# Row-free SSM quantities ahead of the first product, the norm's factors by a product with ones, and a plain second feed-forward product

## The chip, the cores and the metric

One core of one Trainium2 chip runs the whole kernel. The metric is the device time of one launch in microseconds (us); a figure given for a kernel is the median of its runs.

## What is computed

One layer of a hybrid encoder, on 512 rows of width 1024 in fp32: three residual sub-layers. Cut to what matters here:

```python
h = rms_norm(x, norm_mix_g)                    # 512 x 1024
p = h @ w_in                                   # q | k | v | conv input (512) | u (256)
o_sb   = stick_breaking_attention(q, k, v)     # 8 heads of 64
o_conv = conformer_conv(p[..., s3:s4], ...)
o_ssm  = s5_ssm(p[..., s4:], lam_re, lam_im, log_dt, b, c, d, glu_w)
x = x + mixed @ w_out
x = x + memory_cross_attention(rms_norm(x), rms_norm(mem), ...)
hf = rms_norm(x, norm_ffn_g)
gate, up = split(hf @ ffn_w_in)                # hidden width 2816
x = x + (silu(gate) * up) @ ffn_w_out          # 2816 -> 1024
```

In `s5_ssm` many quantities do not depend on the rows: the step `dt`, the decay `exp(lam dt)` with its powers, sines and cosines, and the discretised input matrix `bb` made of `fr`, `fi` and b. They depend on the parameters alone. The state scan and the outputs then use them with u.

## The kernel before

**Products.** Every large product is made in three TensorE instructions (`mm3`, L104 to L108): each operand is split into a high part, cast by ScalarE (ACT, L112), and a low part, subtracted by VectorE (DVE, L113), and high x high, high x low and low x high are summed in a PSUM bank. `load_w` (L87 to L95) fetches weights into one of three `wst` buffers and splits them in the same way (cast L93, subtraction L94).

**Order.** The order on each engine comes from a scheduler that follows the order of the program and the priorities given (`tc.high_priority`), and from pools: a tile with a tag waits until the buffers of that tag are free. PSUM has eight banks in three tags, `acc` (4), `z` (2) and `tp` (2). The pool of split operands has four buffers of each half (`whi`, `wlo`); the split weight tiles of the feed-forward stage (`wbh`, `wbl`) have two.

**Head.** The four row tiles of x are fetched, normalised by `norm_rows` (L151 to L156: a sum of squares on ACT, a reciprocal root, and at L156 one DVE instruction that multiplies a half row by the root and by `gb`), transposed on TensorE (L165, tiles `nxp`) and split into `xnh` and `xnl`. `gb`, the norm's factors on all 128 partitions, comes by two broadcasting transfers of 256 KB each, issued between those of x (L857 to L861). Then `ssm()` (from L276) is woven by `weave` (L175) with a side chain: the convolution's input product (tiles `cv`, weights `wc0` to `wc3`), the projections for stick-breaking (`qkv`, weights `ws00` and on), and the convolution's taps. The generator `ssm` yields how much side work may go in at each point (`SSM_FILL`). Its own order before: the product for u (weights `wu0`, `wu1`), the transposes `uk` and `UT`, the row-free quantities, then `wr`, `wi`, `Qr`, `Qi` (powers times `bb` and c, L432 and L435), their transposes `wTr`, `wTi` (L446), the small products `kp` (L460) and their copies `Kf` (L464, L467), the products S (L479) and the scan.

**Middle.** Stick-breaking attention, the output projection, cross-attention and the first feed-forward product follow. The last works in 22 units with PSUM sums f...acc, f...tp and f...z on an order written out by hand (L1238). It leaves `aF[p]`, for each of 11 pairs p two hidden tiles of 128 x 512 (hidden x rows).

**Second feed-forward product** (L1250 to L1357). It takes the hidden tiles by pairs p and p + 11, cuts rows and columns into halves, and computes each 2 x 2 block product with seven products in place of eight. `shared(p)` makes four of them for all pairs, `others(p)` the other three in a second pass over the pairs. The combinations of the weights (tiles `foa`, `fob`, `foc`, `keep`) are made on GpSimd (POOL; L1276 to L1278, L1296), those of the hidden values on DVE (L1283 to L1285) and POOL (L1289). The results are added up into `xr` (L1325) by DVE and, for a part, by POOL, and stored.

Of the kernel before, what the change touches and what calls it, by code (L numbers as in the profile page):

```python
# [70 lines left out]
def layer(ctx: ExitStack, tc: tile.TileContext, A: dict, out: bass.AP, dbg=None):  # L71
# [79 lines left out]
    def norm_rows(t, xt, gb, h, hiT, loT, pool, tag, bank="tp"):  # L151

        ss = pool.tile([P, 1], F32, tag="nss", bufs=2, name=f"{tag}ss{t}")
        s.activation(h, xt, AF.Square, accum_out=ss)
        r = rstd(ss, D, pool, 1, "rn")
        rows_turn(t, h, hiT, loT, tag, bank, lambda c: v.scalar_tensor_tensor(h[:, c], xt[:, c], r, gb[:, c], op0=ALU.mult, op1=ALU.mult))  # L156
# [119 lines left out]
    def ssm(sp, sk, wu):  # L276
        def sc(name):
            o, n = SK[name]
            return sk[:, o:o + n]
# [6 lines left out]


        uT = sp.tile([P, 2, LC, NCH], F32, tag="uT", name="uT")
        pu = [ps("acc", f"u{ct}") for ct in range(2)]
        for h in range(2):  # L290
            c = slice(h * 256, h * 256 + 256)
            for ct in range(2):
                for k in range(KD):
                    o = (k % 4) * 256 + ct * P
                    mm3(pu[ct][:, c], cols(wu[k // 4], slice(o, o + P)), [x[:, k, c] for x in xn], k == 0, k == KD - 1)
        for ct in range(2):
            s.copy(uT[:, ct].rearrange("p j c -> p c j"), pu[ct].rearrange("p (c j) -> p c j", j=LC))

        uk = sp.tile([P, NST, LC, 32], F32, tag="wTr", name="uk")
        UT = sp.tile([P, NST, NCH], F32, tag="UT", name="UT")  # L300
        for ct in range(2):
            pt = ps("tp", f"uk{ct}")
            for j in range(LC):
                te.transpose(pt[:, j * P:(j + 1) * P], uT[:, ct, j, :], ident)
            v.tensor_copy(uk[:, ct * 4:ct * 4 + 4], pt.rearrange("p (j t h) -> p t j h", j=LC, h=32))
        for hf in range(2):
            pt = ps("tp", f"UT{hf}")
            for k in range(4):
                T = hf * 4 + k
                te.transpose(pt[:, k * P:(k + 1) * P], uk[:, T].rearrange("p j h -> p (j h)"), ident)  # L310
            s.copy(UT[:, hf * 4:hf * 4 + 4, :].rearrange("p t c -> p (t c)"), pt)

# [81 lines left out]
        yield SSM_FILL[0]  # L394
# [25 lines left out]
        v.tensor_tensor(bb[:, 1], b1, b2, op=ALU.add)  # L420
        halves = [(slice(i * 64, i * 64 + 64), slice(i * 16, i * 16 + 16)) for i in range(2)]
# [426 lines left out]
    with tc.tile_pool(name="ssmp", bufs=1, side="right") as sp:  # L848
        sk = sp.tile([P, NSK], F32, name="sk")
        xb = [slotB("xb" + i, F32, i, 1).rearrange("p (a b) t -> p a (b t)", a=2) for i in "hl"]  # L850
        gb = sp.tile([P, D], F32, tag="wTi", name="gb")
# [5 lines left out]
        for i in range(2):  # L857
            c = slice(i * 512, i * 512 + 512)
            nc.sync.dma_start(gb[:, c], A["norm_mix_g"][c].partition_broadcast(P))
            if i == 0:  # L860
                x_rows(1)  # L861
        nc.sync.dma_start(sk, A["sk"])
        wu = [load_w(A["w_u"][:, 4 * i:4 * i + 4, :].rearrange("p k n -> p (k n)"), 1024, f"wu{i}") for i in range(2)]
# [23 lines left out]
        weave(ssm(sp, sk, wu), side)  # L887
# [152 lines left out]
    with tc.tile_pool(name="ff", bufs=1, side="right") as ff:  # L1040
# [207 lines left out]


        HF = NF // 2  # L1250
        kp = [slotA("kpa", F32, "h"), slotB("kpb", F32, "h", 0)]
        keep = [kp[p // 8][:, p % 8, :] for p in range(HF)]
        uw = slotB("uw", F32, "l", 0)

        def raw_w(p, nm):
            if p // 2 % 2 == 0:
                return ff.tile([P, 3, 512], F32, tag="wsb", bufs=2, name=nm)
            return slotB(nm, F32, "hl"[p % 2], 1)

        def w_tiles(nm):  # L1260
            return [ff.tile([P, 3, 512], F32R, tag="wb" + i, bufs=2, name=f"{nm}{i}") for i in "hl"]

        def thin(nm, w, src):

            n = src.shape[-1]
            parts = [wp.tile([P, 1024], F32R, tag="w" + i, bufs=WB, name=nm + i)[:, :w * n].rearrange("p (w n) -> p w n", n=n) for i in ("hi", "lo")]
            split(*parts, src)
            return parts

        def shared(p):  # L1270
            r = raw_w(p, f"foa{p}")
            bx = wp.tile([P, 1024], F32, tag="wst", bufs=3, name=f"fob{p}")
            b, x = bx[:, :512], bx[:, 512:].rearrange("p (w n) -> p w n", n=256)
            nc.sync.dma_start(r[:, :3:2, :], A["w_fo"][p].rearrange("p (j n) -> p j n", j=2))
            nc.sync.dma_start(b, A["w_fo"][p + HF][:, 512:])
            g.tensor_tensor(r[:, 1], r[:, 2], r[:, 0], op=ALU.subtract)  # L1276
            g.tensor_tensor(r[:, 2], b, r[:, 2], op=ALU.subtract)  # L1277
            g.tensor_tensor(keep[p], b, r[:, 1], op=ALU.subtract)  # L1278
            W = w_tiles(f"fow{p}")
            split(*W, r[:, :3])  # L1280
            T2 = thin(f"fot{p}", 1, keep[p].unsqueeze(1))
            a = aF[p]
            v.tensor_tensor(x[:, 0], a[:, 1], a[:, 3], op=ALU.add)  # L1283
            v.tensor_tensor(x[:, 1], a[:, 0], a[:, 1], op=ALU.subtract)
            v.tensor_tensor(a[:, 1], x[:, 0], a[:, 0], op=ALU.subtract)  # L1285
            X = [wp.tile([P, 4, 256], F32R, tag="w" + i, bufs=WB, name=f"foy{p}{i}") for i in ("hi", "lo")]
            split(*[y[:, :2] for y in X], a[:, :2])
            split(*[y[:, 2:] for y in X], x)
            g.tensor_tensor(a[:, 0], a[:, 2], a[:, 1], op=ALU.subtract)  # L1289
            at = lambda i: [y[:, i] for y in X]  # L1290
            return [(at(0), [y[:, 0] for y in W]), (at(1), [y[:, 0] for y in T2]), (at(2), [y[:, 1] for y in W]), (at(3), [y[:, 2] for y in W])]

        def others(p):
            r = raw_w(p + 1, f"foc{p}")
            nc.sync.dma_start(r[:, :2, :], A["w_fo"][p + HF].rearrange("p (j n) -> p j n", j=2))
            g.tensor_tensor(r[:, 2], r[:, 0], keep[p], op=ALU.subtract)  # L1296
            W = w_tiles(f"foz{p}")
            split(*W, r[:, :3])
            a = aF[p]
            X = [wp.tile([P, 1024], F32R, tag="w" + i, bufs=WB, name=f"fov{p}{i}") for i in ("hi", "lo")]  # L1300
            X0 = [y[:, :256] for y in X]
            X1 = [y[:, 256:768].rearrange("p (w n) -> p w n", n=256) for y in X]
            split(*X0, a[:, 0])
            split(*X1, a[:, 2:])
# [110 lines left out]
```

## Time and profile before

| | |
|---|---|
| median of 3 runs | 868.52 us (866.0 to 869.06) |
| the profiled execution | 867.2 us |
| its span, first to last instruction | 865.1 us |
| mean granted TensorE clock | 0.960 |
| bytes moved by DMA | 79.49 MB |

One execution was profiled. PE is TensorE's matrix work, PEld its weight loads, which overlap it; DVE, ACT and POOL are VectorE, ScalarE and GpSimd; SP issues the transfers. A window's row gives busy times in a stretch of the span; a row of waits gives the engine and line that waited and what ended the wait; a row of the timeline gives start, duration, engine, line, output and inputs, and in brackets the idle time before it and what ended that.

The stages lie in the span about so: head and SSM to about 130 us, stick-breaking attention to 260 us, then output projection, cross-attention and the first feed-forward product, and the second feed-forward product from 718.5 us to the end.

### The profile page before, as it was taken

The page shows a single profiled execution, that of the slowest core. Times are in us where ns is not written, and L with a number is a line of the kernel's source. Part 1 is how long each engine was busy: PE and PEld are TensorE (multiplying, and loading weights), DVE is VectorE, ACT ScalarE, POOL GpSimd, SP SyncE. Part 2 cuts the span into 40 slices and gives each one's busy share as a digit, 9 for nine tenths or more (in the row PEclk, how much of TensorE's full clock was granted, in tenths as well). Part 3 has the DMA queues.
Part 4 walks back from the last instruction along what each step waited for, and adds up shares of the span by engine and source line. Part 5 has one row for each costly group of instructions (what it writes and reads, how often), then busy time and mean ns, then how long its engine had stood idle before and what let it go on. Part 6 is the DMA issues. An engine that isn't in the chain of part 4 may idle for free.

```text
span 865.1 us, 12277 instructions
## 1 busy us (share of the span) xinstructions
PE 782.9 (90%) x4570; PEld 679.5 (79%) x4570; DVE 747.0 (86%) x1173; ACT 421.5 (49%) x764; POOL 295.4 (34%) x211
## 2 busy tenths in 40 slices
PE   5969999798789999999999689999999997787888
PEld 4758897685567778888888589999999995565676
DVE  6989999999697958575847997999999899999995
ACT  6423546476676746345634553434343333434542
POOL 3550000000000000000000636677777656788850
PEclk9989999898798999999999989999999999899999
DMA  7300221132420432420341122333332223232141
GB/s 258 96 27 1 73 73 56 43 122 89 136 68 25 124 120 88 133 73 25 123 146 49 46 76 99 102 118 99 122 123 98 86 74 122 73 110 82 65 158 74
DMA packets 25659, 79.49 MB, mean 92 GB/s; under 512 B 2816, under 2 KB 3072, under 8 KB 25600
## 3 DMA queue, kind: packets, MB, share of 16 engines
q1 hardware_dynamic: 25600, 78.71, 27.8%
q8 instruction: 36, 0.59, 0.3%
q14 instruction: 23, 0.19, 0.1%
HBM read 76.60 MB, written 2.10 MB: 91 GB/s over the span
## 4 chain that ended last, share of the span: by engine, by line
PE 59%; DVE 24%; POOL 5%; ACT 5%; issue 3%; DMA 3%; SPq 0%; DVEq 0%; POOLq 0%; ACTq 0%
PE xo L106 2%; PE xo L108 2%; PE xo L107 2%; PE f L107 2%; PE f L106 2%; PE f L108 2%; PE xq L106 2%; PE xq L108 2%; PE xq L107 2%; PE qkv L107 2%; POOL foa L1277 2%; PE qkv L108 2%; PE qkv L106 1%; POOL foa L1276 1%; DVE ss L694 1%
## 5 line engine op out<-in xcount | busy, mean ns | idle before, releaser
L732 POOL TENSOR_TENSOR sqa<-sqa,sq 128x512 f32<-128x512 f32 x3 | 3.9, 1286 | 255.2 <-ACT sq L731 221.6
L1124 POOL TENSOR_TENSOR wgb<-wga,wgb 128x512 f32<-128x512 f32 x22 | 42.0, 1909 | 141.5 <-DMA wga<-in_w_gu_dram 136.6
L1123 POOL TENSOR_TENSOR wgb<-wgb 128x512 f32<-128x512 f32 x20 | 35.2, 1762 | 40.8 <-DMA wgb<-in_w_gu_dram 32.0
L583 DVE SCALAR_TENSOR_TENSOR cac<-hp,pk,cac 128x512 f32<-128x512 f32 x60 | 44.4, 748 | 0.0
L1188 POOL TENSOR_TENSOR aF<-aF,fup 128x1024 f32<-128x1024 f32 x10 | 34.8, 3478 | 4.2 <-DVE fup L1184 4.2
L1140 POOL TENSOR_TENSOR wga<-wga 128x512 f32<-128x512 f32 x20 | 27.5, 1376 | 20.4 <-DVE wga L1139 20.4
L1289 POOL TENSOR_TENSOR aF<-aF 128x256 f32<-128x256 f32 x11 | 20.4, 1854 | 15.8 <-DVE foy0lo L113 4.4
L1139 DVE TENSOR_TENSOR wga<-wgb,wga 128x512 f32<-128x512 f32 x22 | 22.3, 1015 | 0.1
L1276 POOL TENSOR_TENSOR foa<-foa 128x512 f32<-128x512 f32 x11 | 17.6, 1601 | 11.2 <-DMA foa<-in_w_fo_dram 11.2
L681 PE MATMUL z<-kh,qh 64*128 64x512 f32 (+3 forms) x32 | 14.6, 456 | 7.1 <-DVE ss L695 7.1
L1277 POOL TENSOR_TENSOR foa<-fob,foa 128x512 f32<-128x512 f32 x11 | 19.7, 1794 | 0.2
L696 ACT ACTIVATE ss<-ss 128x384 f32<-128x384 f32 (+1 forms) x24 | 13.5, 562 | 12.8 <-DVE ss L695 11.9
L689 ACT ACTIVATE sa<-z 128x384 f32<-128x384 f32 (+1 forms) x24 | 12.7, 530 | 13.3 <-PE z L684 13.2
L681 PEld LDWEIGHTS z<-kh,qh 64*128 64x128 f32 x32 | 6.6, 205 | 15.4 <-DVE ss L695 6.5
L113 DVE TENSOR_TENSOR wTl<-wT,wTh 128x384 fp32r<-128x384 f32 (+2 forms) x40 | 16.4, 416 | 2.1 <-ACT wTh L112 2.0
L1186 ACT ACTIVATE aF<-aF 128x1024 f32<-128x1024 f32 x11 | 11.6, 1056 | 13.2 <-DVE aF L1182 11.0
L1296 POOL TENSOR_TENSOR foc<-foc,kpa 128x512 f32<-128x512 f32 x8 | 15.7, 1975 | 5.8 <-DMA foc<-in_w_fo_dram 4.6
L112 ACT CAST wTh<-wT 128x384 fp32r<-128x384 f32 (+2 forms) x40 | 14.7, 371 | 5.7 <-PE wT L708 3.5
L692 DVE SCALAR_TENSOR_TENSOR sa<-z,sa 128x384 f32<-128x384 f32 (+1 forms) x24 | 14.3, 597 | 3.5 <-ACT sa L691 3.3
L694 DVE TENSOR_TENSOR_SCAN ss<-ones,sa 128x512 f32<-128x512 f32 (+1 forms) x16 | 17.3, 1083 | 0.0
L708 PE MATMUL wT<-ident,ss 128*128 128x128 f32 x80 | 13.6, 291 | 1.6 <-DVE ql L116 1.4
L1283 DVE TENSOR_TENSOR fob<-aF 128x256 f32<-128x256 f32 x11 | 14.4, 1308 | 0.1
(2309 smaller groups left out, 3452.5 us busy)
## 6 DMA issues: line engine op xcount, KB each, us to landing
wgb<-in_w_gu_dram SPq DMA_DIRECT2D x22, 512.0 KB, 3.3
wga<-in_w_gu_dram SPq DMA_DIRECT2D x22, 512.0 KB, 3.4
foa<-in_w_fo_dram SPq DMA_DIRECT2D x11, 512.0 KB, 3.7
foc<-in_w_fo_dram SPq DMA_DIRECT2D x11, 512.0 KB, 3.3
fob<-in_w_fo_dram SPq DMA_DIRECT2D x11, 256.0 KB, 3.3
xr<-in_x_dram SPq DMA_DIRECT2D x4, 512.0 KB, 7.4
out_dram<-xr SPq DMA_DIRECT2D x8, 256.0 KB, 2.1
xbh<-in_x_dram SPq DMA_DIRECT2D x2, 512.0 KB, 5.0
```

Of the source, the lines that this page charges most:

```text
L106: te.matmul(o, a[0], b[0], start=start, stop=False)
L107: te.matmul(o, a[0], b[1], start=False, stop=False)
L108: te.matmul(o, a[1], b[0], start=False, stop=stop)
L583: v.scalar_tensor_tensor(a, x, w, a, op0=ALU.mult, op1=ALU.add)
L694: v.tensor_tensor_scan(ts[:, ::-1], d0, ta[:, ::-1], 0.0, op0=ALU.mult, op1=ALU.add)
L1123: eng.tensor_tensor(b[:, 0], b[:, 1], b[:, 2], op=ALU.add)
L1124: g.tensor_tensor(b[:, 1], a[:, 0], b[:, 1], op=ALU.subtract)
L1139: v.tensor_tensor(a[:, 0], b[:, 0], a[:, 0], op=ALU.subtract)
L1140: eng.tensor_tensor(a[:, 1], a[:, 1], a[:, 0], op=ALU.subtract)
L1188: (g if i + 1 < len(units) else v).tensor_tensor(aF[p], aF[p], dst, op=ALU.mult)
L1276: g.tensor_tensor(r[:, 1], r[:, 2], r[:, 0], op=ALU.subtract)
L1277: g.tensor_tensor(r[:, 2], b, r[:, 2], op=ALU.subtract)
```

## The change

Three parts.

1. **The factors.** `gb` is no longer broadcast by transfers. The 1024 factors come in one row (`grow`, 4 KB), and two matmuls of a column of ones with that row (`onesr`) spread it over 128 partitions into two PSUM banks of tag `acc`. L156 reads its factor from there. The transfers are issued in the order grow, first row tile, sk (the SSM's parameters), second row tile, wu0, wu1, third and fourth row tile; before it was first row tile, gb, second row tile, gb, sk, wu0, wu1, and the rest.
2. **The row-free quantities.** In `ssm` they stand ahead of u's product, and the generator is run to that point (`next(S5)`) right after the calls of `norm_rows`. Two tiles change their tags with it (`tmpm`, `onesr`).
3. **The second feed-forward product** becomes plain: 22 hidden tiles, eight sums of 128 rows x 512 columns in all eight PSUM banks, each hidden tile used in all of them in turn; for the last two hidden tiles sum by sum, with its addition into `xr` and its store right behind. The pairs, combinations and the second pass are gone.

```diff
-        rows_turn(t, h, hiT, loT, tag, bank, lambda c: v.scalar_tensor_tensor(h[:, c], xt[:, c], r, gb[:, c], op0=ALU.mult, op1=ALU.mult))
+        rows_turn(t, h, hiT, loT, tag, bank, lambda c: v.scalar_tensor_tensor(
+            h[:, c], xt[:, c], r, gb[c.start // 512] if isinstance(gb, list) else gb[:, c], op0=ALU.mult, op1=ALU.mult))
...
     def ssm(sp, sk, wu):
-        uT = sp.tile([P, 2, LC, NCH], F32, tag="uT", name="uT")
...
-        yield SSM_FILL[0]
...
         v.tensor_tensor(bb[:, 1], b1, b2, op=ALU.add)
+        yield 0
+
+        uT = sp.tile([P, 2, LC, NCH], F32, tag="uT", name="uT")
...
+        yield SSM_FILL[0]
...
-        gb = sp.tile([P, D], F32, tag="wTi", name="gb")
+        grow = sp.tile([1, D], F32, tag="wTi", name="grow")
+        onesr = sp.tile([1, P], F32, tag="t3", name="onesr")
+        v.memset(onesr, 1.0)
+        nc.sync.dma_start(grow, A["norm_mix_g"].unsqueeze(0))
+        gps = [ps("acc", f"gb{i}") for i in range(2)]
+        for i in range(2):
+            te.matmul(gps[i], onesr, grow[:, i * 512:i * 512 + 512], start=True, stop=True)
...
-                norm_rows(t, xb[t // 2][:, t % 2, :], gb, hn[t], xn[0], xn[1], sp, "nx", ("tp", "z")[t % 2])
+                norm_rows(t, xb[t // 2][:, t % 2, :], gps, hn[t], xn[0], xn[1], sp, "nx", ("tp", "z")[t % 2])
         dbg("xn", xn)
+        S5 = ssm(sp, sk, wu)
+        next(S5)
...
+        slots = [("acc", t, 0) for t in range(4)] + [("z", 0, 1), ("z", 1, 1), ("tp", 2, 1), ("tp", 3, 1)]
+        acc = {(t, hf): ps(tag, f"fo{t}{hf}") for tag, t, hf in slots}
+        TAIL = 2
+
+        def hidden(k):
+            p, j = k // 2, k % 2
+            X = [wp.tile([P, 1024], F32R, tag="w" + i, bufs=WB, name=f"fox{k}{i}")[:, :512] for i in ("hi", "lo")]
+            split(*X, aF[p][:, 2 * j:2 * j + 2].rearrange("p a t -> p (a t)"))
+            r = wp.tile([P, 1024], F32, tag="wst", bufs=3, name=f"for{k}")
+            nc.sync.dma_start(r, A["w_fo"][p + j * (NF // 2)])
+            W = [ff.tile([P, 3, 512], F32R, tag="wb" + i, bufs=2, name=f"fow{k}{i}").rearrange("p a n -> p (a n)")[:, :1024] for i in "hl"]
+            split(*W, r)
+            return X, W
+
+        def step(k, X, W, t, hf):
+            mm3(acc[t, hf], cols(X, slice(t * P, (t + 1) * P)), cols(W, slice(hf * 512, hf * 512 + 512)), k == 0, k == NF - 1)
+
+        for k in range(NF - TAIL):
+            ops = hidden(k)
+            for _, t, hf in slots:
+                step(k, *ops, t, hf)
+        ops = [hidden(k) for k in range(NF - TAIL, NF)]
+        for _, t, hf in slots:
+            for k in range(TAIL):
+                step(NF - TAIL + k, *ops[k], t, hf)
+            c = slice(hf * 512, hf * 512 + 512)
+            v.tensor_tensor(xr[:, t, c], acc[t, hf], xr[:, t, c], op=ALU.add)
             nc.sync.dma_start(out[t * P:(t + 1) * P, c], xr[:, t, c])
```

The first place is the start of the program on PE. The names `hnVr`, `hnVi`, `hnKf` and `hnUT` are the four normalised row tiles, `nxp` their transposes, u the SSM's input product. Before, the last two rows of the transposes of the first two row tiles and the start of u:

```order
L165 MATMUL nxp_150<-ident,hnVr 128x128
L165 MATMUL nxp_178<-ident,hnVi 128x128
L106 MATMUL u_260<-xnh,wu0h 128x256
L106 MATMUL u_261<-xnh,wu0h 128x256
L107 MATMUL u_260<-xnl,wu0h 128x256
L108 MATMUL u_260<-xnh,wu0l 128x256
```

And with the change:

```order
L862 MATMUL gb_109<-grow,onesr 128x512
L862 MATMUL gb_110<-grow,onesr 128x512
L166 MATMUL nxp_147<-ident,hnVr 128x128 x4
L166 MATMUL nxp_155<-ident,hnVr 128x128 x4
L166 MATMUL nxp_175<-ident,hnVi 128x128 x4
L166 MATMUL nxp_183<-ident,hnVi 128x128 x4
L166 MATMUL nxp_203<-ident,hnKf 128x128 x4
L106 MATMUL u_421<-xnh,wu0h 128x256
L106 MATMUL u_422<-xnh,wu0h 128x256
L166 MATMUL nxp_231<-ident,hnUT 128x128 x4
L107 MATMUL u_421<-xnl,wu0h 128x256
```

The two products that spread the factors (`gb`) stand first, the transposes of the first half of the third row tile now stand ahead of u's first matmul, and those of the fourth lie between u's matmuls.

The second place is DVE in the SSM, from the building of `Qr` to the scan; `ws02l` is the low half of a weight tile for the projections, `csg` a step of the convolution's gate, t are scratch tiles. Before:

```order
L94 TENSOR_TENSOR ws02l<-ws02s,ws02h 128x768
L435 TENSOR_TENSOR Qr<-t_521,t_522 64x8x4x16 x2
L432 TENSOR_TENSOR t_521<-ncr,api 128x512
L432 TENSOR_TENSOR t_522<-sk,apr 128x512
L435 TENSOR_TENSOR Qi<-t_521,t_522 64x8x4x16 x2
L483 TENSOR_TENSOR t_522<-S_697,E 128x512
L484 TENSOR_TENSOR t_523<-S_697,E 128x512
L144 SCALAR_TENSOR_TENSOR csg_800<-cv_592,csg_800 128x512
L467 SCALAR_TENSOR_TENSOR Kf<-ident,sk,Kf 128x128 x4
```

And with the change, from the split of `ws02` on, which now has `Qr` and `Qi` ahead of it (the lines are 5 further down):

```order
L94 TENSOR_TENSOR ws02l<-ws02s,ws02h 128x768
L472 SCALAR_TENSOR_TENSOR Kf<-ident,sk,Kf 128x128 x4
L487 TENSOR_TENSOR t_382<-S_697,E 128x512
L472 SCALAR_TENSOR_TENSOR Kf<-ident,sk,Kf 128x128 x4
L488 TENSOR_TENSOR t_383<-S_702,E 128x512
L489 TENSOR_TENSOR t_384<-S_702,E 128x512
L490 TENSOR_TENSOR t_385<-S_697,E 128x512
L491 TENSOR_TENSOR Vr<-t_382,t_383 128x512
L492 TENSOR_TENSOR Vi<-t_384,t_385 128x512
L495 SCALAR_TENSOR_TENSOR Vr<-r_266,Vr 128x128
L495 SCALAR_TENSOR_TENSOR Vi<-r_266,Vi 128x128
L144 SCALAR_TENSOR_TENSOR csg_805<-cv_597,csg_805 128x512
```

The split of `ws02` went from ahead of `Qr` to behind `Qi`, and `Kf` ahead of the first product with S; the step of `csg` comes further down, behind the scan's first rows.

The third place is DVE in the second feed-forward product; `fow` are the split weights, `fot`, `foy` and `fox` split operands, `fob` and `aF` hidden values. Before, for one pair in the first pass:

```order
L113 TENSOR_TENSOR fot4lo<-kpa,fot4hi 128x512
L1283 TENSOR_TENSOR fob_7554<-aF_6078 128x256
L1284 TENSOR_TENSOR fob_7554<-aF_6078 128x256
L1285 TENSOR_TENSOR aF_6078<-fob_7554,aF_6078 128x256
L113 TENSOR_TENSOR foy4lo<-aF_5602,foy4hi 128x512
L113 TENSOR_TENSOR fow4l<-foa_7455,fow4h 128x1536
L113 TENSOR_TENSOR foy4lo<-fob_7456,foy4hi 128x512
L113 TENSOR_TENSOR fot5lo<-kpa,fot5hi 128x512
```

And with the change, for four hidden tiles:

```order
L113 TENSOR_TENSOR fox3lo<-aF_4893,fox3hi 128x512
L113 TENSOR_TENSOR fox4lo<-aF_5131,fox4hi 128x512
L113 TENSOR_TENSOR fow2l<-for_7333,fow2h 128x1024
L113 TENSOR_TENSOR fox5lo<-aF_5131,fox5hi 128x512
L113 TENSOR_TENSOR fow3l<-for_7367,fow3h 128x1024
L113 TENSOR_TENSOR fox6lo<-aF_5369,fox6hi 128x512
L113 TENSOR_TENSOR fow4l<-for_7401,fow4h 128x1024
```

Each hidden tile has two DVE rows, its own split of 128x512 and that of its weights of 128x1024, and nothing is combined. `fox` stands two tiles or more ahead of `fow`.

More of the change, by code (lines that the diff above doesn't have):

```diff
@@ L285, in small @@
             return sp.tile([P, *(shape or (NST,))], F32, name=name)
-        uT = sp.tile([P, 2, LC, NCH], F32, tag="uT", name="uT")
[L289 to L311, printed above, removed]
         NA = 8
@@ L856, in layer @@
         x_rows(0)
[L857 to L861, printed above, removed]
         nc.sync.dma_start(sk, A["sk"])
+        x_rows(1)
         wu = [load_w(A["w_u"][:, 4 * i:4 * i + 4, :].rearrange("p k n -> p (k n)"), 1024, f"wu{i}") for i in range(2)]
@@ L886, in layer @@
         side = chain(conv_gemm(), along(sb_proj(0), T, 2), along(sb_proj(1), T, 2))
-        weave(ssm(sp, sk, wu), side)
+        weave(S5, side)
         drain(side)
@@ L1246, in layer @@
         dbg("x3", xr)
[L1250 to L1304, printed above, removed]
-            return [([y[:, 0] for y in X1], [y[:, 0] for y in W]), (X0, [y[:, 1] for y in W]), ([y[:, 1] for y in X1], [y[:, 2] for y in W])]
@@ L1307, in second @@
-        def second(ops, banks, done, then=iter(())):
-            n = len(banks)
-            acc = [[ps(tag, f"fo{n}{i}{tt}") for tt in range(2)] for i, tag in enumerate(banks)]
-            for p in range(HF):
-                x = ops(p)
-                if p > 1:
-                    next(then, None)
-                for i, (a, w) in enumerate(x):
-                    for tt in range(2):
-                        mm3(acc[i][tt], [y[:, tt * P:(tt + 1) * P] for y in a], w, p == 0, p == HF - 1)
-                        if p == HF - 1:
-                            done(i, tt, acc[i][tt])
@@ L1344, in shared_rest @@
-        def shared_rest():
-            for t, c, x in rest:
-                add(t, c, x, g)
-                if t > 1 and c == last:
-                    store(t, c)
-                yield
-        def others_done(i, tt, acc):
-            t, c = ((tt, first), (tt, last), (2 + tt, first))[i]
-            add(t, c, acc)
-            store(t, c)
-        second(shared, ("acc", "z", "tp", "acc"), shared_done)
-        second(others, ("acc", "z", "tp"), others_done, shared_rest())
+        slots = [("acc", t, 0) for t in range(4)] + [("z", 0, 1), ("z", 1, 1), ("tp", 2, 1), ("tp", 3, 1)]
```

42 lines of the change are left out of this document (23 added, 19 removed).

## The prediction

> **What bounds the kernel now.** The page comes first: the busy line of each engine and the forty slices of 21.6 us.
>
> ```profile
> span 865.1 us, 12277 instructions
> PE 782.9 (90%) x4570; PEld 679.5 (79%) x4570; DVE 747.0 (86%) x1173; ACT 421.5 (49%) x764; POOL 295.4 (34%) x211
> PE   5969999798789999999999689999999997787888
> DVE  6989999999697958575847997999999899999995
> POOL 3550000000000000000000636677777656788850
> PEclk9989999898798999999999989999999999899999
> ```
>
> PE is the bound almost everywhere. The two stretches that this change rewrites are exceptions. In slices 1 to 4 PE has gaps while DVE is full, and in the last seven slices PE stands at 7 or 8 beside a DVE at 9 and a busy POOL. The windows view puts numbers on those stretches (columns: stretch, length, busy us of PE, PEld, DVE, ACT, POOL with instruction counts, granted clock, DMA share, GB/s).
>
> ```profile
> 5.60:60.00 54.40, 40.56 (x231) 35.07 (x232) 50.50 (x133) 25.19 (x53) 27.85 (x48) 0.95 0.40 137
> 600.00:700.00 100.00, 100.00 (x844) 100.00 (x844) 96.00 (x115) 42.21 (x45) 66.66 (x35) 1.00 0.31 102
> 716.80:857.90 141.10, 114.92 (x466) 89.00 (x466) 134.05 (x122) 60.22 (x80) 98.07 (x55) 0.95 0.27 94
> 722.00:803.00 81.00, 61.53 (x234) 47.11 (x233) 80.59 (x70) 30.02 (x41) 67.62 (x39) 0.92 0.29 99
> 803.00:857.90 54.90, 49.37 (x210) 38.71 (x210) 48.25 (x45) 25.65 (x33) 29.32 (x16) 1.00 0.25 87
> ```
>
> The head (first row) is bound by DVE: it is idle 54.40 - 50.50 = 3.9 us out of 54.4. The first feed-forward product (second row) is bound by PE: 100 of 100 us. The second feed-forward product (the other rows) is bound by DVE in its first part, 80.59 of 81 us busy, while PE works 61.53. Over the whole stage PE is idle 141.10 - 114.92 = 26.2 us.
>
> **The second feed-forward product.** Its ends and its step come from the timeline of PE (columns: start, duration, engine and line, output and inputs).
>
> ```profile
> 718.50 0.28 PE L108 MATMUL f101acc<-hfbh,wt101lo 128*128 128x256 f32 x1
> 719.86 0.50 PE L106 MATMUL fo<-fow0h,foy0hi 128*128 128x512 f32 x1 [1.08 <-ACT foy0hi L112]
> ...
> 853.02 0.39 PE L107 MATMUL fo<-foz9l,fov9hi 128*128 128x512 f32 x1
> ...
> 856.91 0.39 PE L106 MATMUL fo<-foz10h,fov10hi 128*128 128x512 f32 x1
> ...
> 860.80 0.40 PE L108 MATMUL fo<-foz10h,fov10lo 128*128 128x512 f32 x1
> ```
>
> From the start of the last f matmul to the start of the last fo matmul are 860.80 - 718.50 = 142.3 us. Between 853.02 and 856.91 lie 17 steps with nothing missing: 3.89 / 17 = **0.229 us** for a 512-column matmul when all is ready. The old stage issues (4 + 3) products x 2 x 3 x 11 = 462 of them; 462 x 0.229 = 105.8 us. The other 36.5 us are waits and matmuls at a lower clock (0.92 from 722 to 803). The waits of PE there name the cause (engine and line, what it waited for: us in total, times, longest):
>
> ```profile
> PE fo L107 <- DVE fow2l L113: 4.4, 1, 4.4
> PE fo L107 <- DVE fow7l L113: 2.7, 1, 2.7
> ```
>
> PE waits for DVE to make the low half of a weight tile that POOL combined first. The change takes out every POOL combination and the three DVE combinations per pair, and pays with plain products: 22 hidden tiles x 8 accumulators x 3 = 528 matmuls, 66 more. At 0.229 us that is **120.9 us**, if PE never waits. For that each tile must be ready in time. The prices:
>
> ```profile
> L113 DVE TENSOR_TENSOR fot0lo<-kpa,fot0hi x1: 687/687/687, 719.3 to 719.3; 128x512 fp32r<-128x512 f32 x1
> L1132 DVE TENSOR_TENSOR wt40lo<-wga,wt40hi x1: 1215/1215/1215, 578.1 to 578.1; 128x1024 fp32r<-128x1024 f32 x1
> L1132 DVE TENSOR_TENSOR wt51lo<-wga,wt51hi 128x1024 fp32r<-128x1024 f32 x1 | 2.3, 2320 | 0.0
> L1131 ACT CAST wt00hi<-wga x1: 1054/1054/1054, 488.7 to 488.7; 128x1024 fp32r<-128x1024 f32 x1
> L112 ACT CAST fov0hi<-aF x2: 406/512/617, 800.5 to 800.8; 128x256 fp32r<-128x256 f32 x1, 128x512 fp32r<-128x512 f32 x1
> foc<-in_w_fo_dram SPq DMA_DIRECT2D x11, 512.0 KB, 3.3
> ```
>
> Per hidden tile PE works 24 x 0.229 = 5.5 us. DVE needs 0.69 (hidden values) + 1.22 (weights) = 1.9 us, ACT 0.62 + 1.05 = 1.7 us, and the weights are one 512 KB transfer of 3.3 us with three buffers to land in. The tightest place is the ring of two split weight tiles: tile k+2 may be cast only once PE is through with k, and then PE has 5.5 us of k+1. One X split ahead of it in each queue included, the chain is ACT 0.62 + 1.05, DVE 0.69 (largely beside the cast) + 1.22: at most 3.6 us. 1.9 us of slack is the cover, and if DVE ran at 2.32 instead of 1.22, as it did once while POOL worked beside it, 4.7 us would still fit. A wait for the transfer is covered by three landing buffers: it starts two tiles, some 11 us, ahead. So I take no wait inside, and 0.3 us from the last f matmul to the first fo (1.36 before, with a 1.08 wait for an X that is now cast ahead). The last steps, one evacuating DVE add and one store, are the same as before: nothing. **Term: 120.9 + 0.3 - 142.3 = -21.1 us.** Bounds: -22 if the start costs nothing; if the clock stands at 0.95, as it did over the old stage, 528 x 0.229 / 0.95 = 127.3, so -15.
>
> One rule speaks against this part. The Trainium skill, page "TensorE: Matmul & The Clock Gate", section "A second HAM failure mode: psum-queue depth-cycling", says that a kernel which cycles through PSUM banks in each iteration idles often enough to fall out of full clock again and again, and that its 512-column matmuls had a median of 379 ns. The new stage does cycle, through eight banks per hidden tile; by that figure it would be an estimated 528 x 0.379 = 200 us. The rows do not agree: the old stage from 803 to 857.9 cycles six banks in the same way and shows a granted clock of 1.00 and 0.229 us. The measurement decides; what the rule leaves is the last rival below.
>
> **The head.** The rows of this part, from the timelines of DVE and PE and the waits of PE:
>
> ```profile
> 8.91 0.75 DVE L156 SCALAR_TENSOR_TENSOR hnVr<-xbh,rny,gb 128x512 f32<-128x512 f32 x1 [1.31 <-DMA gb<-in_norm_mix_g_dram]
> 60.48 0.69 DVE L483 TENSOR_TENSOR t<-S,E 128x512 f32<-128x512 f32 x1
> 62.98 0.69 DVE L144 SCALAR_TENSOR_TENSOR csg<-cv,csg 128x512 f32<-128x512 f32 x1 [1.21 <-ACT csg L143]
> 66.36 1.14 DVE L467 SCALAR_TENSOR_TENSOR Kf<-ident,sk,Kf 128x128 f32<-128x128 f32 x4 [2.70 <-ACT Kf L464]
> ...
> 13.77 0.77 PE L106 MATMUL u<-xnh,wu0h 128*128 128x256 f32 x2
> 20.38 0.60 PE L165 MATMUL nxp<-ident,hnKf 128*128 128x128 f32 x4
> 66.39 1.16 PE L479 MATMUL S<-UT,wTr 128*128 128x128 f32 x8 [0.18 <-ACT Kf L464]
> ...
> PE nxp L165 <- DVE hnVr L156: 7.7, 1, 7.7
> PE wTr L446 <- DVE wr L435: 3.5, 1, 3.5
> PE wTi L446 <- DVE wi L435: 2.3, 1, 2.3
> PE kp L460 <- DVE Qr L435: 2.3, 1, 2.3
> ```
>
> *The factors.* Two 256 KB broadcasts become a 4 KB transfer and two plain fp32 products. The nearest row is S: eight instructions that fill a 512-column bank take 1.16 us, so the two cost about 2.3. They stand ahead of the first transpose, and PE waits 7.7 us there for the first normalised rows: hidden. DVE now reads its factor from PSUM; csg, which reads PSUM too, takes 0.69 against 0.75 for the old form, so that costs nothing. The wait of 1.31 for the second broadcast goes. If the cover failed, 2.3 us would come late into the head.
>
> *The moved quantities.* The DVE and POOL instructions free of the rows are the same ones as before, only earlier in the program. DVE, the bound, does no less. What can be won is idle time: the 3.9 us before 60, and the 1.21 and 2.70 behind. By the order, the Kf copies on ACT and the Kf steps on DVE now come ahead of csg, and the split of ws02 behind Qi, so the 1.21 for csg should go. The three stalls of PE (3.5, 2.3, 2.3) shorten only as far as DVE is earlier. What can be lost is on PE: transposes of the third row tile now stand ahead of u, and those of the fourth in its midst, so u starts not at 13.77 but behind where the first of those ran, 20.38 + 0.60 = 21.0, that is 7.2 us late. Before, PE filled the wait for later rows with u; now it will have both at once. What hides it: u is needed for the S products, and DVE takes up the first of those only at 60.48; until then it has other work, whatever PE does. If that cover is gone, up to 7.2 us come in. The bounds are therefore **+7.2 and -7.8** (3.9 + 1.21 + 2.70). I take the two waits that the moved rows remove by name, 1.31 + 1.21: **-2.5 us**, near the middle, because the two ends come from different engines and the bound one, DVE, has no term on the losing side.
>
> The stages between (stick-breaking, attention, first feed-forward product) get the same instructions in nearly the same order: nothing, apart from what a DVE that is ahead may bring (first rival).
>
> **Sum.** 867.2 (the profiled execution, of which 865.1 is its span) - 21.1 - 2.5 = 843.6. The median of the three runs, 868.5, lies 1.3 above that execution: **845.0 us**.
>
> **The rivals.** Rows for them:
>
> ```profile
> PE z L681 <- DVE ss L695: 7.1, 5, 4.4
> 59.08 0.63 PE L108 MATMUL cv<-xnh,wc3l 128*128 128x512 f32 x1
> 59.50 0.63 PE L106 MATMUL cv<-xnh,wc3h 128*128 128x512 f32 x1
> ...
> 742.94 1.77 DVE L113 TENSOR_TENSOR fot3lo<-kpa,fot3hi 128x512 fp32r<-128x512 f32 x1
> ```
>
> *A DVE that is ahead brings more.* In the stick-breaking stage PE waits 7.1 us for DVE (first row). If the head hands over DVE work earlier, as the moved csg would, those go too: 845.0 - 7.1 = **837.9**. For it: DVE is full in the slices before. Against it: the chain through ss is in series, and its start depends on PE's projections.
>
> *The late u is not covered.* The head gives +7.2 in place of -2.5: 867.2 - 21.1 + 7.2 + 1.3 = **854.6**. For it: PE is busy 40.56 of the 54.4 us, and cannot catch up as easily as DVE's slack suggests. Against it: the three stalls, 8.1 us together, lie behind u and could take it in.
>
> *The plain stage is not free of waits, so the change does not do what it says.* If DVE's splits stay slow (2.32 for the weights, 1.77 for X by the last row) and two X stand ahead in the queue, the chain is 1.05 + 2 x 1.77 + 2.32 = 6.9 against 5.5 us: 22 x 1.4 = 31 us at most, and half of that by a middling speed, 15 to 20 us, which eats most of the term: 867.2 - 21.1 + 20 - 2.5 + 1.3 = **about 865**. Against it: POOL has no work in that stage, and it was only beside POOL that such a split took 2.3.
>
> *The other side: the clock.* The new stage is pure matmul count, so it depends on the granted clock as the old one did not. The two cv rows are a 512-column product after PE had been idle: 0.42 us a step. At that step the stage takes 528 x 0.42 = 222 us: 867.2 + 80 - 2.5 + 1.3 = **about 945**. It decides from 142.3 / 528 = 0.270 us a step on, a mean clock of 0.85. For it: 0.92 in the old stage. Against it: the 0.92 came with the waits, and 600 to 700 us ran full at 1.00.
>
> **How the numbers follow.** The forecast of 845 (with 841 to 850 for itself: a stage clock a little below 1, the head at nothing or double) gets 0.58; the DVE that is ahead 0.18; the late u 0.14; the waits that stay 0.06; the clock 0.04. A range of 834 to 856 takes in the first three with the bounds of the head's term and leaves out 0.10, and some of the edges. About 0.5%, 4.3 us, is what a measurement of this kernel can tell from no change: the first three cases are faster by more, the waits that stay lie mostly within 0.5%, the clock is slower. So 0.91, 0.05, 0.04.
>
> **What would show it.** Where the head ends, PE goes over to the projections of the stick-breaking stage:
>
> ```profile
> 76.43 0.33 PE L106 MATMUL qkv<-ws00h,xnh 128*128 128x384 f32 x1
> ```
>
> In the profile after: the span from the last f matmul to the last fo matmul 121 to 122 us with PE at 9 in every slice and a step of 0.229; no POOL there; no PE wait for a fow over 0.5 us. If waits for fow remain, the ring step was wrong; if the steps are longer at a granted clock under 0.95, the clock step. In the head: no DVE wait for a DMA of the factors; u starting near 21 us; the start of qkv between 69 and 78 in place of 76.4; later than 78 would make the cover of u wrong. In the stick-breaking stage: the 7.1 us wait for ss kept.

## The result and the profile after

The changed kernel takes **845.27 us** (median of 4 runs, 844.17 to 847.63) against 868.15 us (866.0 to 869.06): a ratio of 0.9744, 95% interval 0.9716 to 0.9771. The forecast was 845.0. The profiled execution of the changed kernel is the slowest of its four, 847.6 us with a span of 845.6; this matters below.

The page of the changed kernel, busy times and slices of 21.1 us:

```profile
span 845.6 us, 12171 instructions
PE 794.1 (94%) x4640; PEld 693.2 (82%) x4640; DVE 651.1 (77%) x1100; ACT 396.5 (47%) x729; POOL 191.6 (23%) x150
PE   5969999899799999999999959999999999999998
DVE  6889989899888967756766799899999987433333
POOL 3560000000000000000001275577676662000000
```

PE's last seven digits went from 7 and 8 to 9 (8 in the very last slice). DVE fell there from 9 to 4 and 3 (7 in the first of the seven), and POOL, which had 5 to 8 in six of them, is idle behind the first. The window over the second feed-forward product (columns: stretch, length, busy us of PE, PEld, DVE, ACT and POOL with counts, granted clock, DMA share, GB/s) and four rows of PE's timeline:

```profile
718.20:842.00 123.80, 123.50 (x531) 99.58 (x530) 45.61 (x52) 30.99 (x39) 0.00 (x0) 1.00 0.27 90
```

```profile
718.26 0.28 PE L108 MATMUL f101acc<-hfbh,wt101lo 128*128 128x256 f32 x1
718.38 0.40 PE L106 MATMUL fo<-fow0h,fox0hi 128*128 128x512 f32 x1
...
830.38 0.40 PE L106 MATMUL fo<-fow20h,fox20hi 128*128 128x512 f32 x1
...
841.30 0.40 PE L108 MATMUL fo<-fow21h,fox21lo 128*128 128x512 f32 x1
```

From the last f matmul to the last fo matmul are 841.30 - 718.26 = 123.0 us, where 142.3 were. Only 123.80 - 123.50 = 0.3 us of it is idle, and the granted clock is 1.00 throughout. The head reads otherwise. The projections of the stick-breaking stage start later than before, at 79.71 and not at 76.43, and yet the last f matmul starts at about the same time in both traces, 718.50 and 718.26:

```profile
79.71 0.33 PE L106 MATMUL qkv<-ws00h,xnh 128*128 128x384 f32 x1
```

By these two traces alone the head gives nothing and the stage all of it. Over several runs that turned out to be wrong.

### The profile page after: what moved, and what is told of

Its sections match the earlier page's. It is cut to its first block, busy times and chain, and to the rows that moved or that the text cites. A ratio compares the mean times of both kernels' runs of the same rounds, so it can differ in the third digit from the quotient of the medians.

```text
span 845.6 us, 12171 instructions
## 1 busy us (share of the span) xinstructions
PE 794.1 (94%) x4640; PEld 693.2 (82%) x4640; DVE 651.1 (77%) x1100; ACT 396.5 (47%) x729; POOL 191.6 (23%) x150
## 4 chain that ended last, share of the span: by engine, by line
PE 77%; DVE 15%; ACT 4%; issue 2%; DMA 1%; POOL 1%; SPq 0%; DVEq 0%; POOLq 0%; ACTq 0%
PE fo L106 5%; PE fo L107 5%; PE fo L108 5%; PE f L107 2%; PE f L106 2%; PE f L108 2%; PE xo L106 2%; PE xo L108 2%; PE xo L107 2%; PE qkv L108 2%; PE qkv L107 2%; PE xq L106 2%; PE xq L108 2%; PE xq L107 2%; PE qkv L106 2%
## 5 line engine op out<-in xcount | busy, mean ns | idle before, releaser
L1133 POOL TENSOR_TENSOR wgb<-wga,wgb 128x512 f32<-128x512 f32 x22 | 41.8, 1901 | 141.6 <-DMA wga<-in_w_gu_dram 136.6
L1148 DVE TENSOR_TENSOR wga<-wgb,wga 128x512 f32<-128x512 f32 x22 | 23.1, 1050 | 0.2
L700 DVE TENSOR_TENSOR ss<-z,ss 128x384 f32<-128x384 f32 (+1 forms) x24 | 14.2, 593 | 0.0
L695 ACT ACTIVATE sa<-sa 128x384 f32<-128x384 f32 (+1 forms) x24 | 13.5, 562 | 0.4
L696 ACT ACTIVATE sa<-sa 128x384 f32<-128x384 f32 (+1 forms) x24 | 13.5, 561 | 0.3
L773 DVE SCALAR_TENSOR_TENSOR xr<-wo,rb,xr 128x512 f32<-128x512 f32 x16 | 11.7, 744 | 1.7 <-PE wo L108 1.6
L713 PEld LDWEIGHTS wT<-ident,ss 128*128 128x128 f32 x80 | 9.2, 144 | 4.5 <-DVE ql L116 1.9
```

The source lines that it names most:

```text
L713: te.transpose(pt[:, b * P:(b + 1) * P], ts[:, b * P:(b + 1) * P], ident)
L1133: g.tensor_tensor(b[:, 1], a[:, 0], b[:, 1], op=ALU.subtract)
L1148: v.tensor_tensor(a[:, 0], b[:, 0], a[:, 0], op=ALU.subtract)
```

## The experiments

Two theories stood at the start. **The plain product is all of it**, as the two traces say. **The two parts add**, with a head worth 2.5 us as predicted, and the first trace of the changed kernel is a slow draw. The rival of both: the late u costs something that the factors pay back.

**1 to 4: the parts apart.** Each of these kernels has the plain second product. The first has the head as before:

```diff
-        gps = [ps("acc", f"gb{i}") for i in range(2)]
...
+            nc.sync.dma_start(gb[:, c], A["norm_mix_g"][c].partition_broadcast(P))
...
-        S5 = ssm(sp, sk, wu)
-        next(S5)
...
-        weave(S5, side)
+        weave(ssm(sp, sk, wu), side)
```

Inside `ssm`, u's product stands ahead of the row-free quantities again, in this kernel and in the next.

> The plain second feed-forward product alone, with the head as it was before (factors broadcast by transfers, u's product first). Theory 'the plain product is all of it': the head's two waits that went (1.31 and 1.21 us of DVE) were replaced by others, so this gains as much as the whole change, 845 to 846 us, and its last stage takes 122 to 123 us from the first fo matmul to the last. Rival 'the head gives its 2.5 us': this is 2 to 3 us slower than the whole change, 847.5 to 848.5.

The second has the factors by a product but u first, as before:

```diff
-        S5 = ssm(sp, sk, wu)
-        next(S5)
...
-        weave(S5, side)
+        weave(ssm(sp, sk, wu), side)
```

> Plain second product and the factors spread by the product with ones, but u's product ahead of the row-free quantities as before. Theory 'the plain product is all of it': 845 to 846 us, and the 1.31 us wait of DVE for the second broadcast is gone all the same. Rival 'the head gives its 2.5 us, half of it by the factors': about 1.3 us under the plain product alone.

The third has the row-free quantities first, but the broadcasts:

```diff
-        gps = [ps("acc", f"gb{i}") for i in range(2)]
...
+            nc.sync.dma_start(gb[:, c], A["norm_mix_g"][c].partition_broadcast(P))
```

> Plain second product and the row-free quantities ahead of u, but the factors broadcast by transfers as before. Theory 'the plain product is all of it': 845 to 846 us; the stick-breaking projections start later than the 76.4 us of before (78 to 80) and the stage after it makes that up. Rival 'the late u costs and the factors pay for it': 1 to 3 us above the plain product alone.

The fourth is the changed kernel again.

> The changed kernel once more, beside the three others. Expected 845 us. Of its first trace two things are asked again: the step of 0.2333 us in the second product (0.229 in the kernel before), which theory 'the step belongs to the run' would put nearer to 0.229 in this execution and theory 'the step belongs to the program' at 0.2333 again, and the start of the stick-breaking projections, 79.7 us.

**5: the head alone**, with the old second product.

> The changed head (factors by a product with ones, row-free quantities first) with the second feed-forward product as it was before, in seven products. Theory 'the two parts add': the head is worth what the runs with the plain product gave, 849 - 846 = 3 us, so 864 us against 867 for the kernel before. Rival 'the head pays only beside the plain product': within 1 us of the kernel before.

| run | median us (lowest to highest) | ratio to before, 95% |
|---|---|---|
| before (runs 1 to 4) | 867.08 (864.4 to 869.52) | |
| plain_only | 848.93 (848.37 to 850.03) | 0.9796 (0.9773 to 0.9819) |
| factors_plain | 849.08 (848.39 to 852.25) | 0.9803 (0.9776 to 0.9830) |
| rowfree_plain | 846.77 (845.84 to 847.47) | 0.9770 (0.9748 to 0.9793) |
| after_again | 845.97 (844.17 to 847.32) | 0.9759 (0.9733 to 0.9785) |
| head_only (before 866.75) | 863.80 (858.19 to 866.36) | 0.9964 (0.9946 to 0.9982) |

The plain product gives 867.08 - 848.93 = 18.2 us. The head gives 848.93 - 845.97 = 3.0 us beside it and 866.75 - 863.80 = 3.0 beside the old product (1.6 to 4.7 by the interval): the two parts add. "The plain product is all of it" falls. Of the head, moving the row-free quantities gives 2.2 (848.93 - 846.77). The rival had this kernel slower than plain_only, but u is not late in it: it starts at 14.65 us, and at 18.24 and 18.78 in the two traces of the changed kernel, which is no slower for it. So no cost of a late u is seen. The factors alone give nothing (849.08), and the 0.8 they seem to add to the other part is inside the scatter.

Why one trace could mislead is seen in a window that runs from 5.6 us to the first matmul of the cross-attention's weights (xa_wk). Four rows, in the order before, plain_only, the changed kernel's first trace, its second trace. Before:

```profile
5.60:257.78 252.18, 218.73 (x1161) 184.17 (x1161) 227.11 (x467) 139.49 (x295) 29.15 (x49) 0.94 0.27 86
```

The plain product alone:

```profile
5.60:258.93 253.33, 220.17 (x1160) 185.01 (x1161) 226.97 (x465) 139.40 (x293) 29.15 (x49) 0.92 0.27 86
```

The changed kernel, first trace:

```profile
5.60:257.90 252.30, 220.27 (x1162) 187.22 (x1161) 226.93 (x465) 139.59 (x294) 32.63 (x58) 0.93 0.27 83
```

The changed kernel, second trace:

```profile
5.60:255.06 249.46, 220.06 (x1162) 186.99 (x1161) 226.73 (x465) 139.77 (x293) 32.12 (x58) 0.92 0.26 84
```

DVE's busy time is the third one behind the length: 227 us of work in all four, to 0.4. Length less work is its idle time: 25.1, 26.4, 25.4 and 22.7 us. DVE's work does not change, so whatever makes these first 258 us shorter shows as idle time of DVE that is gone. Two executions of one and the same changed kernel differ by 2.7 us in it (span 845.6 and 842.6), all of it ahead of 80 us, and by almost nothing after it; in both the second product takes 122.92 us between its first and last matmul.

The traces of all the experiments, those further down too, can be taken together, since four of them have the head as before (before, plain_only and runs 7 and 8) and seven have the changed head (the changed kernel twice, head_only and runs 9 to 12). DVE's idle time in them, in us:

| | 5.6 to 80 | 80 to 130 | 130 to xa_wk | together | xa_wk starts at |
|---|---|---|---|---|---|
| head as before, 4 traces | 8.0 to 9.1 | 2.4 to 4.0 | 14.1 to 15.0 | 25.1 to 27.6, median 26.2 | 257.8 to 260.0, median 258.8 |
| changed head, 7 traces | 5.7 to 8.3 | 2.5 to 4.2 | 12.8 to 13.0 | 22.7 to 25.4, median 23.1 | 255.1 to 257.9, median 255.6 |
| rowfree_plain, 1 trace | 6.1 | 3.4 | 14.3 | 23.8 | 256.6 |
| factors_plain, 1 trace | 8.4 | 5.0 | 16.6 | 29.9 | 262.6 |

The head is worth 3.2 us by these medians, 3.0 by the runs, and the first trace of the changed kernel is the latest of its seven. The gain is in two places, ahead of 80 us and behind 130 us; rowfree_plain has the first of them alone. The trace of factors_plain is the slowest of its four runs (852.25 us) and says little about their median. The one trace of head_only doesn't show the two parts by itself: its span is 4.1 us shorter than that of before, but 2.5 of it lie in the old second product (139.8 against 142.3 us).

Which waits went and came is seen in DVE's waits (who waited, for whom, total us, times, longest). Between 5 and 80 us, the changed kernel's second trace:

```profile
DVE rnm L126 <- ACT hnVr L154: 4.6, 1, 4.6
DVE Kf L472 <- ACT Kf L469: 2.8, 1, 2.8
DVE xnl L113 <- ACT xnh L112: 1.1, 1, 1.1
```

And factors_plain:

```profile
DVE rnm L126 <- ACT hnVr L154: 4.7, 1, 4.7
DVE xnl L113 <- ACT xnh L112: 2.8, 1, 2.8
DVE Kf L468 <- ACT Kf L465: 2.2, 1, 2.2
```

And two rows of the changed kernel's first trace:

```profile
DVE xnl L113 <- ACT xnh L112: 2.1, 2, 1.9
DVE ws02l L94 <- ACT ws02h L93: 1.3, 1, 1.3
```

The wait for the broadcast factors (1.3 us before) and that for csg (1.2) are gone in all seven traces with the changed head, where the four with the old one have 2.1 to 3.3 us of the two together. The wait for the cast of the transposed rows (xnl) grew, from 0.4 to 0.8 us in those four to 1.1 to 2.4 in the seven; in factors_plain it is 2.8. DVE getting earlier to a step for which ACT has not yet made the cast would explain this, and row-free work placed ahead would fill such a wait; no run shows it wait by wait.

Behind 130 us, before:

```profile
DVE xr L768 <- DMA xr<-in_x_dram: 1.8, 1, 1.8
```

This wait for x, fetched again for the sum with the output projection, is 1.3 to 2.0 us in the four traces with the old head and at most 0.2 in the seven with the changed one. Other waits there came and went beside it, and what each is worth is not told apart.

**6: u earlier.** Is the late u covered? Built on experiment 11 below (kick), which has the same head as the changed kernel.

```diff
         for h in range(2):
+          with tc.high_priority(offset=(3600, 0)[h]):
```

> The run 'kick' with the first half of u's product raised in priority, so that only one transpose of the third row tile stands ahead of it on TensorE, and the first 48 matmuls of u come before the other transposes. Theory 'DVE bounds the head and the late u is covered': no gain, 842 to 844 us as 'kick', since DVE's idle time up to the cross-attention's weights stays at 22 to 25 us; it may even lose where the last row tiles come later to DVE. Rival 'the late u costs': 2 us or more under 'kick', 840.5 or less.

It takes 847.38 us (847.07 to 850.23), ratio 0.9792 (0.9774 to 0.9809), against 842.69 for the same kernel without it: no gain, a loss of 4.7 us by the medians and 5.9 by the two ratios to before (0.9792 and 0.9724). Its second product is as long as that kernel's, to 0.01 us. The row of the window for it, and then for the kernel without the early u:

```profile
5.60:259.96 254.36, 223.37 (x1161) 188.91 (x1161) 226.72 (x465) 139.38 (x293) 31.08 (x58) 0.91 0.26 82
```

```profile
5.60:255.56 249.96, 220.08 (x1161) 186.91 (x1161) 226.90 (x465) 139.66 (x294) 31.66 (x58) 0.92 0.26 84
```

DVE's idle time is 27.64 against 23.06 us, 4.6 more, of which 1.8 lie ahead of 80 us and 3.0 behind 130 us. (The spans, 845.6 and 843.5, differ by less, because the trace of kick loses 2.2 us in the first feed-forward product.) The run does not hold u's time alone: u's first matmul comes 1.1 us earlier than in kick, at 17.64, but its last one 1.7 later, at 34.22, and the first product with S starts at 63.47 in place of 57.40. So it shows that this order is worse, and not why.

**7 and 8: what made the old stage wait.** The kernel before, with POOL's combinations left out: five per pair, four in the first pass and one in the second. The slots are loaded instead, and the split that took `keep[p]` takes `b`:

```diff
-            g.tensor_tensor(r[:, 1], r[:, 2], r[:, 0], op=ALU.subtract)
-            g.tensor_tensor(r[:, 2], b, r[:, 2], op=ALU.subtract)
-            g.tensor_tensor(keep[p], b, r[:, 1], op=ALU.subtract)
+            nc.sync.dma_start(r[:, 1], A["w_fo"][p][:, :512])
...
-            g.tensor_tensor(a[:, 0], a[:, 2], a[:, 1], op=ALU.subtract)
...
-            g.tensor_tensor(r[:, 2], r[:, 0], keep[p], op=ALU.subtract)
+            nc.sync.dma_start(r[:, 2], A["w_fo"][p][:, 512:])
```

> The kernel before, with its second feed-forward product in seven products, but the combinations on POOL (four per pair) left out: the slots that they filled are loaded instead, so its output is another. Matmuls, casts, splits and DVE combinations stay. Theory 'POOL's work, and DVE slowed beside it, made the waits': a 512-column split takes 0.69 us in place of 1.77, DVE needs 5 us per pair of the first pass against 5.5 us of PE, and the stage takes 106 to 112 us in place of 142.3. Rival 'DVE's own work was too much': DVE stays full and the stage over 125 us.

The second has the same, with as many combinations of the same sizes on POOL into `keep[p]`, which nobody reads:

```diff
+            g.tensor_tensor(keep[p], r[:, 2], r[:, 0], op=ALU.subtract)
+            g.tensor_tensor(keep[p], b, r[:, 2], op=ALU.subtract)
+            g.tensor_tensor(keep[p], b, r[:, 1], op=ALU.subtract)
...
+            g.tensor_tensor(keep[p][:, :256], a[:, 2], a[:, 1], op=ALU.subtract)
...
+            g.tensor_tensor(keep[p], r[:, 0], r[:, 1], op=ALU.subtract)
```

> The kernel before with the second product in seven products, the combinations left out as in the run without POOL (its output is another), but POOL makes as many combinations of the same sizes from the same tiles into a buffer that nobody reads. So DVE has POOL beside it and nobody waits for POOL's results. Theory 'DVE slowed beside POOL makes the waits': most of the way back to 142, 130 us or more, with 512-column splits of 1.7 us. Theory 'the wait for POOL's own chain makes them': near the 110 us of the run without POOL, under 118.

The window over the stage and two DVE rows, without POOL's work:

```profile
720.30:830.40 110.10, 106.95 (x463) 86.31 (x462) 88.94 (x115) 55.99 (x74) 11.03 (x6) 1.00 0.48 166
```

```profile
741.21 0.69 DVE L113 TENSOR_TENSOR fot5lo<-fob,fot5hi 128x512 fp32r<-128x512 f32 x1
```

And with POOL at work aside:

```profile
720.60:866.50 145.90, 118.92 (x465) 92.86 (x463) 136.57 (x121) 56.00 (x74) 92.42 (x58) 0.91 0.39 130
```

```profile
762.88 1.78 DVE L113 TENSOR_TENSOR fot5lo<-fob,fot5hi 128x512 fp32r<-128x512 f32 x1
```

110.1 us against 145.8 between the first and last fo matmul (836.8 and 873.2 us in all, one run each), where the kernel before has 140.9. In both runs no cast, split or matmul waits for a combination of POOL, and the loads of the second wait for it 1.7 us in all; in the kernel before ACT waited for them, up to 9.3 us for one. DVE's busy time goes from 88.9 to 136.6 us of the windows for nearly the same work (115 and 121 records), the same split takes 0.69 and 1.78 us, and the clock falls to 0.91 with the waits. Inside the second run the same is seen while POOL waits 5.5 us for a transfer, from 755.0 to 760.5 us:

```profile
756.57 0.68 DVE L113 TENSOR_TENSOR foy3lo<-fob,foy3hi 128x512 fp32r<-128x512 f32 x1
...
760.52 1.88 POOL L1277 TENSOR_TENSOR kpa<-foa 128x512 f32<-128x512 f32 x1 [5.49 <-DMA foa<-in_w_fo_dram]
...
761.17 1.79 DVE L113 TENSOR_TENSOR foy4lo<-fob,foy4hi 128x512 fp32r<-128x512 f32 x1
```

It is not POOL's results that made the stage long, but DVE, slowed beside POOL. This is what the Trainium skill says, page "SBUF — State Buffer", section "Who interferes with whom": a DVE instruction with two SBUF inputs contends with a GpSimd instruction that reads SBUF. The traces here agree and give the price, 2.6 times for this form.

The first run also shows what seven products would be worth if they cost POOL nothing: 110 us, 13 under the plain stage. It is no kernel for use, since without the combinations its output is another.

**9 and 10: how much cover the plain stage has.** The low half of each weight tile made N more times:

```diff
             split(*W, r)
+            for _ in range(N):
+                v.tensor_tensor(W[1], r, W[0], op=ALU.subtract)
```

> The changed kernel with the low half of each split weight tile of the second product made three times in place of once (2 x 1.23 us more of DVE per hidden tile, 54 us in all). Theory 'the ring of two has a slack': in the trace of the changed kernel a low half is ready 2.8 us before PE comes to the tile, so 2.5 us more fit, and the stage stays at 123 us from the first to the last fo matmul (under 126). Rival 'DVE sets the step': 1 us and more per hidden tile, over 143 us.

> The changed kernel with the low half of each split weight tile of the second product made five times (4 x 1.23 us more of DVE per hidden tile). Theory 'the ring of two has a slack of 2.8 us': the chain is 2.1 us too long, and DVE itself needs 0.69 + 5 x 1.23 = 6.8 us per hidden tile against 5.6 of PE, so the stage grows by 20 x 1.2 = 24 us or more, to 145 to 155. Rival 'there is far more slack': still under 130.

In the changed kernel a weight tile is ready 2.8 us ahead of its use (753.55 + 1.23 = 754.78 against 757.58):

```profile
753.55 1.23 DVE L113 TENSOR_TENSOR fow7l<-for,fow7h 128x1024 fp32r<-128x1024 f32 x1 [0.26 <-ACT fow7h L112]
```

```profile
757.58 0.40 PE L106 MATMUL fo<-fow7h,fox7hi 128*128 128x512 f32 x1
```

With two more (2.5 us) PE has no wait; with four (4.9 us) it has one, mostly of 0.9 us, at nearly every tile. The windows over the stage, first N = 2, then N = 4:

```profile
715.70:838.70 123.00, 123.00 (x530) 99.38 (x528) 96.16 (x92) 30.98 (x39) 0.00 (x0) 1.00 0.27 88
```

```profile
716.20:862.70 146.50, 127.75 (x530) 98.65 (x528) 141.15 (x132) 31.00 (x39) 0.00 (x0) 0.99 0.21 71
```

123.0 and 146.5 us (844.6 and 870.3 in all, one run each). The cover is real: 2.5 us more per tile cost nothing. The second run does not show where the ring's slack ends, because DVE alone then needs 6.8 us per tile against 5.6 of PE, and is busy 141.15 of 146.5 us.

**11 and 12: the step.** Over 480 steps of the changed kernel one step is (830.38 - 718.38) / 480 = 0.2333 us, and it was the same in every trace of the plain stage that had no waits; the kernel before had 0.229. One small product with zeros behind the second tile's first product:

```diff
+        zero = ff.tile([P, 3, 512], F32R, tag="wsb", bufs=2, name="zero")[:, 0, :P]
+        g.memset(zero.bitcast(F32), 0.0)
...
+                if k == 1 and (t, hf) == (0, 0):
+                    te.matmul(acc[t, hf][:, :P], zero, ops[1][0][:, :P], start=False, stop=False)
```

> The changed kernel with one small product with a tile of zeros (128 columns, added into the first sum) behind the first of the eight products of the second hidden tile. The step of the second product was 0.2333 us in every trace of the changed kernel, and about 0.229 behind its only wait of 0.2 us, near the end. Theory 'the even step of 0.2333 is a state of the running pipeline that an irregular step ends': about 0.229 from there on, the stage 2 us shorter, 121 us from the first to the last fo matmul, and the whole 844. Rival 'the step belongs to the operands and the order of the sums': 123 us as before.

And the three matmuls of a product in another order:

```diff
+            te.matmul(acc[t, hf], x[1], w[0], start=k == 0, stop=False)
+            te.matmul(acc[t, hf], x[0], w[0], start=False, stop=False)
+            te.matmul(acc[t, hf], x[0], w[1], start=False, stop=k == NF - 1)
```

> The changed kernel with the three matmuls of a product of the second feed-forward stage in another order: low x high first, then high x high and high x low. Theory 'the step is a state of the running pipeline': no telling, either of 0.2333 and 0.229, but even. Theory 'the step belongs to the order of the three': a step other than 0.2333. Rival 'nothing in the order matters': 0.2333 and 122.9 us.

Four tile starts of the first, two of them ahead of the extra product and two, 432 steps apart, behind it:

```profile
718.17 0.40 PE L106 MATMUL fo<-fow0h,fox0hi 128*128 128x512 f32 x1
...
723.77 0.40 PE L106 MATMUL fo<-fow1h,fox1hi 128*128 128x512 f32 x1
...
729.41 0.39 PE L106 MATMUL fo<-fow2h,fox2hi 128*128 128x512 f32 x1
...
828.29 0.39 PE L106 MATMUL fo<-fow20h,fox20hi 128*128 128x512 f32 x1
```

Ahead of it the step is (723.77 - 718.17) / 24 = 0.2333 us, behind it (828.29 - 729.41) / 432 = 0.2289, and the stage takes 121.0 us from the first to the last fo matmul in place of 122.9. In the other order the step is again 0.2333 (tile 20 starts 112.00 us behind tile 0). A wait seems to do the same as the extra product. In the run with N = 4, behind a wait of 0.88 us, 14 steps take 757.27 - 754.06 = 3.21 us, 0.229 each:

```profile
753.72 0.50 PE L107 MATMUL fo<-fow5l,fox5hi 128*128 128x512 f32 x1 [0.88 <-DVE fow5l L1272]
754.06 0.40 PE L108 MATMUL fo<-fow5h,fox5lo 128*128 128x512 f32 x1
...
757.27 0.39 PE L108 MATMUL fo<-fow5h,fox5lo 128*128 128x512 f32 x1
```

The kernel with the extra product takes **842.69 us** (840.35 to 845.51, ratio 0.9724, 0.9700 to 0.9748), the lowest median of the kernels that compute the whole layer. Of its distance to the changed kernel, 1.9 us is the stage by the traces; the rest is not told from scatter.

## Why the prediction was right

The sign, the size and the mechanism of the main term held. Two terms were a little off, in opposite directions, and the start of the sum was a little high: the median of 868.5 stood for a kernel whose later medians were 867.08, 866.75, 866.42 and 865.75. That 845.0 came out within 1 us of both medians (845.27 and 845.97) is in part luck.

- **The second product: -21.1 predicted, -18.2 measured** by medians, 123.0 against 142.3 = -19.3 by the traces. "I take no wait inside" was right, and so was the start (0.12 us against 0.3). Mis-sized was the step: 0.229 was read from a stretch of the old stage, and the running plain stage has 0.2333, which is 528 x 0.0043 = 2.3 us. That the step could differ for the same form of instruction was not allowed for. The sign "121 to 122 us" was missed with it, by 1 us.
- **The old stage's waits.** The reading that DVE, slowed beside POOL, made them is shown by runs 7 and 8.
- **The ring of two.** "At most 3.6 us" of chain was cautious, and the cover larger than the 1.9 taken: 2.8 us by the trace, and 2.5 us of added work on DVE cost nothing.
- **The head: -2.5 predicted, -3.0 measured, for a reason that was half right.** The 1.21 us for csg and the 1.31 for the factors went, as named, and idle time of DVE is what the gain consists of, as the prediction held when it called the head bound by DVE. But taking away the wait for the factors paid nothing by itself (849.08 against 848.93), some of the time came back as a longer wait for ACT's cast, and moving the row-free quantities alone paid 2.2. The stages between were put at nothing, yet DVE's idle time from 130 us to xa_wk fell by 1.6 (medians 14.6 and 12.9). That the sum comes to about 3 is the right size by terms that are not quite the predicted ones.
- **The late u** (the rival at 854.6). u starts at 18.8, not 21.0, and the cover held: the changed kernel is no slower than rowfree_plain, where u starts at 14.65, and forcing u forward cost 4.7 us. The mark "later than 78 would make the cover of u wrong" was a bad mark: qkv started at 79.7 and 76.9 in two traces of the same kernel, and from there to xa_wk both took 178.2 us, where before took 181.4.
- **The DVE that is ahead** (837.9). The waits for ss stayed: 7.1 us in the page before and 8.0 after. It did not happen.
- **The waits that stay** and **the clock**: neither. The rule of the Trainium skill, page "TensorE: Matmul & The Clock Gate", section "A second HAM failure mode: psum-queue depth-cycling", speaks of a kernel whose TensorE idles briefly between groups of matmuls, and that idling is absent here: the stage cycles eight banks per hidden tile with 0.3 us of idle time in 123.8, at a granted clock of 1.00. The prediction's 200 us took the page's 379 ns for a step, while the page gives it as the median of one matmul at full clock. In this trace one matmul lasts 0.40 us and the next starts 0.2333 us after it, so the two are not the same thing.

## What to carry to other kernels

A scheme that saves matmuls can lose where the engines that prepare its operands slow each other: here 66 matmuls fewer (15 us) cost 36 us of waits and slow clock, and 32 of them went when POOL had no work (142.3 against 110.2). Where one engine bounds a stretch, add up its work and its idle time to a fixed later event; a gain there is idle time that goes, and taking away one wait need not pay. A single trace of before and after is not enough for a term of 3 us when two executions of one kernel differ by 3.

## What was not expected

The same fp32r matmul of 512 columns in a full queue ran at an even 0.2333 us a step for 112 us, and one irregular product of 128 columns brought it to 0.2289 for the rest of the stage, in the same trace and from that place on. Another order of the three matmuls did not. That the step is a state of the running pipeline is what these runs suggest; what the state consists of was not found.
